# Stage changes with two chunks side by side, and three transposes on VectorE and a bounce through DRAM in place of TensorE

## The chip, the cores and the metric

One core of a Trainium2 chip runs the whole program. The metric is the device time of one execution in microseconds (us), smaller is better. It is the median of three executions; one more execution was recorded by the profiler, and all rows below are of that one.

## The reference

One layer of a streaming-encoder block on a sequence of 256 frames of 2048 float32 values. Everything is computed once, batch 1:

```python
h = rms_norm(x); p = h @ W_in                       # 2048 x 6656: [x_m | out gate | u | branch gates]
xc = silu(causal_conv(x_m)); q, k = xc @ Wq, xc @ Wk;  v = x_m @ Wv      # 4 heads of 256
hcell = mlstm(q, k, v, gates(q, k, v))              # matrix memory, max stabiliser
out  = sigmoid(out_gate) * (per_head_rms(hcell) * g + skip * xc)
y_m  = out @ W_up_m                                 # 1024 -> 2048
y    = s5(u); y = gelu(y); y = y * sigmoid(y @ W_glu + b)                # complex diagonal scan, 512 wide
y_s  = y @ W_up_s                                   # 512 -> 2048
x = x + (sigmoid(g_m) * y_m + sigmoid(g_s) * y_s) @ W_out
x = x + (silu(rms(x) @ W_gate) * (rms(x) @ W_up)) @ W_down               # 2048 -> 5632 -> 2048
out = rms_norm(x)
```

## The kernel before

Every large matrix is cut into blocks of 128 rows x 1024 columns (512 KB; two 128-row pieces of a 512-column chunk side by side). `emit_dma` loads a block by the SP queue into `raw` (3 buffers), `emit_split` makes `hi` (ScalarE, the cast of L156) and `lo = raw - hi` (VectorE, L94) of it (3 buffers each), and `o2_block` multiplies: 12 matmuls of 128x512 a block, hi by hi, lo by hi and hi by lo, for both halves (`tt`) of the sequence. The blocks run in one list: w_in in chunks of 8 blocks (`kp` 0 to 7) with the heads' v, q and k between them, the 2 blocks of w_glu inserted three blocks before the end of w_in, then w_up_s (8), w_up_m (16), w_out (32, four chunks), the FFN's gate and up chunks in turn (11 x (8 + 8), from block FFN0 = 168 on), and w_ffn_down (88). From block FFN0+4 on, every fourth block goes to a buffer of another pool, so that its load may be issued well ahead of its turn.

Two generators hold the work beside the blocks. `s5_gen` computes the S5 branch (the scan's products `bu` and `stm`, then `y_mm`, `gelu`, and `ghl`, the hi/lo halves of y). `ml_gen` computes the mLSTM branch (conv, gates, v, the heads, and at its end the output stage that makes `oh`/`ol`, the hi/lo pair that w_up_m multiplies). `pump` steps them between blocks; a yield gives the price by which it paces them. Whoever needs a result calls `until`: `glu_mm` for S5's y before w_glu, `ups_mm` for the GLU's result before w_up_s, `upm_mm` for `out` before w_up_m. After that a scheduler fixes the order of instructions on each engine. An engine takes its instructions strictly in that order.

A change of layout from frames on partitions to channels on partitions is done in two ways. v, the heads' output `hc` and the output gate `so` are transposed by TensorE with an identity (128x128 pieces, into PSUM `aux`). The gate products (`turn`) and the residual (`x1_T`) go by `blocks_T`, a VectorE transpose of 32x32 blocks (L274), and `groups_dma`, which stores the result to a DRAM tile `bounce` (one DMA) and loads it back in another order (four DMAs), all issued by GpSimd (POOL). After each w_out chunk, `x1_T(n)` also prepares `h2h`/`h2l`, that chunk's share of the FFN's left operand; the FFN's `kp` 6 and 7 read the share of chunk 3. In the same way w_out's `kp` 6 and 7 read the share of w_up_m's last chunk.

Of the kernel before, what the change touches and what calls it, by code (L numbers as in the profile page):

```python
# [17 lines left out]
P = 128  # L18
# [29 lines left out]
def block_kernel(ctx: ExitStack, tc: tile.TileContext, d, out):  # L48
# [18 lines left out]
    def u8(shape, dt=F32, name="u"):  # L67
        return up.tile(shape, dt, tag="u8", name=nm(name), bufs=NU8)
# [16 lines left out]
    def aux():  # L85
        return pp.tile([P, 512], F32, tag="aux", name=nm("aux"), bufs=4)
# [6 lines left out]
    def TT(o, a, b, op):  # L93
        return V.tensor_tensor(o, a, b, op=op)  # L94

    def STT(o, a, s, b, op0, op1, **kw):
        return V.scalar_tensor_tensor(out=o, in0=a, scalar=s, in1=b, op0=op0, op1=op1, **kw)  # L97

    def mm(o, l, r, start, stop):
        return PE.matmul(o, l, r, start=start, stop=stop, skip_group_check=True)  # L100
# [8 lines left out]
    def pvs(n, i=None, w=1):  # L109
        a, b = PV[n]  # L110
        if i is None:
            return pv[:, a:b]
        return pv[:, a + i : a + i + w]
# [164 lines left out]
    def groups_dma(dt_, st_):  # L278
# [3 lines left out]
        for j in range(4):  # L282
            nc.gpsimd.dma_start(  # L283
                dt_[32 * j : 32 * j + 32], bounce.rearrange("(i r) j x -> r i j x", i=4)[:, :, j]
            )


    s5 = {}

# [239 lines left out]
    def ml_gen():  # L529
# [38 lines left out]
        vk = u16([P, 2, 2048], name="vk")  # L568
        ml["vk"] = vk
        vtok = vk[:, 0].rearrange("p (a b) -> p a b", a=2)  # L570
        for st in range(2):
            for e4 in range(2):
                ps_ = aux()
                for e in range(4):
                    PE.transpose(ps_[:, e * 128 : e * 128 + 128], vT[:, e4 * 4 + e, st * 128 : st * 128 + 128], ident)
                A.copy(vtok[:, st, e4 * 512 : e4 * 512 + 512], ps_)
                yield 0.05, 0.45, e4
        gt = cp.tile([P, 2, 8], F32, name="gt")


# [5 lines left out]

        def gate_part(i, src, base):
            gs = m2([P, 256])
            nc.gpsimd.memset(gs, 0.0)
            ps_ = aux()  # L590
            for c in range(8):
                r = 32 * (c % 4)
                mm(ps_[r : r + 8, 0:256], wif[:, i * 8 + c, :], src[:, c, :], c < 4, c >= 4)
            for r in range(0, 128, 32):
                A.copy(gs[r : r + 8, :], ps_[r : r + 8, 0:256])
            yield 0.05, 1.2, 1
            pg = aux()
            for tt in range(2):
                mm(pg[:, tt * 8 : tt * 8 + 8], gs[:, tt * 128 : tt * 128 + 128], sel, True, True)
            TT(gt, pg[:, 0:16].rearrange("p (a b) -> p a b", a=2), base, ADD)  # L600
            yield 0.2, 0.4

        yield from gate_part(2, vT, pvs("bif").unsqueeze(1).broadcast_to([P, 2, 8]))
        del vT
        yield 0.2
        xch = u8([P, 8, 256], F32R, name="xch")
        xcl = u8([P, 8, 256], F32R, name="xcl")
# [14 lines left out]
        qT = ml["q"]  # L622
        yield from gate_part(0, qT, gt)
        yield 0.2
        while "k" not in state:
            yield 0
        yield 0.01, 0, 1
# [30 lines left out]
        for hp in range(2):  # L658
# [79 lines left out]
            yield 0.01, 0.65, 1  # L738
            for pT, h in zip(pTs, hh2):
                nps = aux()  # L740
                vs = lambda st: vtok[:, st, h * 256 : h * 256 + 256]
                mm(nps[:, 0:256], pT[:, 0], vs(0), True, True)
                mm(nps[:, 256:512], pT[:, 1], vs(0), True, False)
                mm(nps[:, 256:512], pT[:, 2], vs(1), False, True)
                for tt in range(2):
                    o = hc[:, 2 * h : 2 * h + 2, tt, :]
                    nv = nps[:, tt * 256 : tt * 256 + 256].rearrange("p (a b) -> p a b", a=2)
                    A.activation(o, nv, AF.Copy, scale=dinv[:, h, tt : tt + 1])
                    jk = m2([P, 2, 128])
                    A.activation(jk, o, AF.Square, accum_out=ssh[:, h, tt : tt + 1])  # L750
                yield 0.01, 1.3, 0
# [5 lines left out]
        for h in range(4):  # L757
            for tt in range(2):
                o = hc[:, 2 * h : 2 * h + 2, tt, :]
                A.activation(o, o, AF.Copy, scale=rsh[:, h, tt : tt + 1])  # L760
        yield 0.6, 0, 3
        while "win" not in state:
            yield 0
        so = ml["so"]
        oh = u8([P, 8, 256], F32R, name="oh")
        ol = u8([P, 8, 256], F32R, name="ol")
        for c2 in range(4):
            hps, sps = aux(), aux()
            for src, ps_ in ((hc, hps), (so, sps)):
                for cc in range(2):  # L770
                    for tt in range(2):
                        ct = 2 * c2 + cc
                        c = (cc * 2 + tt) * 128
                        PE.transpose(ps_[:, c : c + 128], src[:, ct, tt, :], ident)  # L774
            t = m2()
            for cc in range(2):
                ct = 2 * c2 + cc
                ts_ = t[:, cc * 256 : cc * 256 + 256]
                A.activation(ts_, xcT[:, ct, :], AF.Copy, scale=pvs("skip", ct))
                STT(ts_, hps[:, cc * 256 : cc * 256 + 256], pvs("mh", ct), ts_, MUL, ADD)  # L780
            TT(t, t, sps, MUL)
            v2 = lambda a: a[:, 2 * c2 : 2 * c2 + 2, :].rearrange("p a b -> p (a b)")
            A.copy(v2(oh), t)
            TT(v2(ol), t, f(v2(oh)), SUB)
            yield 2.1, 0.9, 1
        ml["out"] = (oh, ol)
        state["out"] = 1
        yield 0.1
# [11 lines left out]
    def win_evac(n, acc):  # L800
        if n == 4:
            ud = cp.tile([P, 4, 256], F32, name="s5ud")
            s5["ud"] = ud

            rb = s5["r1b"].rearrange("p (q c) -> p q c", c=16).unsqueeze(1).broadcast_to([P, 2, 16, 16])
            for h in range(2):
                o = ud[:, 2 * h : 2 * h + 2, :].rearrange("p a (q c) -> p a q c", c=16)
                TT(o, acc[h].rearrange("p (a c q) -> p a q c", a=2, q=16), rb, MUL)
            state["u"] = 1
        elif n < 2:  # L810
            if n == 0:
                ml["xm"] = u8([P, 2, 1024], name="xm")
            for tt in range(2):
                A.activation(
                    ml["xm"][:, tt, n * 512 : n * 512 + 512], acc[tt], AF.Copy, scale=r1[:, tt : tt + 1]
                )
            if n == 1:
                state["xm"] = 1
        elif n < 4:
            if n == 2:  # L820
                ml["so"] = u8([P, 8, 2, 128], name="so")
            for tt in range(2):
                A.activation(
                    ml["so"][:, 4 * (n - 2) : 4 * (n - 2) + 4, tt, :],
                    acc[tt].rearrange("p (a b) -> p a b", a=4),
                    AF.Sigmoid,
                    scale=r1[:, tt : tt + 1],
                )
            if n == 3:
                state["so"] = 1  # L830
        else:
            c = n - 5
            key, cc = ("gm", c) if c < 4 else ("gs", c - 4)
            if c == 0:
                mlg.until("heads")
            if cc == 0:
                cur[key] = u16([P, 2, 2048], name=key)
            bg = cur["bg"]
            for tt in range(2):
                o = gate_ap(key, tt, cc)  # L840
                STT(o, acc[tt], r1[:, tt : tt + 1], bg, MUL, ADD)
                A.activation(o, o, AF.Sigmoid)
# [145 lines left out]
    def out_mm(i, nk, hi, lo):  # L988
        n, kp = nk
        if n == 0 and kp == 0:  # L990
            cur["x1"] = u16([P, 2, 2048], name="x1")
            cur["h2h"] = [u8([P, 8, 256], F32R, name="h2h") for _ in range(2)]
            cur["h2l"] = [u8([P, 8, 256], F32R, name="h2l") for _ in range(2)]
        if kp == 0:
            cur["acc"] = [acc_tile(), acc_tile()]
            cs = slice(n * 512, n * 512 + 512)
            with tc.issue_after(wdma[0]):
                nc.sync.dma_start(cur["x1"][:, :, cs], d["x"].rearrange("(a p) c -> p a c", p=P)[:, :, cs])
        o2_block(cur["acc"], lhs_of(cur["mTh"], cur["mTl"], 8), (2 * kp, 2 * kp + 1), hi, lo, kp == 0, kp == 7)
        if kp == 7:  # L1000
            for tt in range(2):
                o = cur["x1"][:, tt, n * 512 : n * 512 + 512]
                TT(o, cur["acc"][tt], o, ADD)
                jk = t2()
                A.activation(jk, o, AF.Square, accum_out=ss2[:, tt, n : n + 1])
            later(lambda: x1_T(n))
# [147 lines left out]
        blocks.insert(len(blocks) - GLU, (d["w_glu"][0, b], glu_mm, (0, b)))  # L1154
    add_mat("w_up_s", 4, 2, ups_mm)
    add_mat("w_up_m", 4, 4, upm_mm)
    add_mat("w_out", 4, 8, out_mm)
    fg, fu = ffn_mm("fg"), ffn_mm("fu")
    FFN0 = len(blocks)
    for n in range(11):  # L1160
        for kp in range(8):
            blocks.append((d["w_ffn_gate"][n, kp], fg, (n, kp)))
        for kp in range(8):
            blocks.append((d["w_ffn_up"][n, kp], fu, (n, kp)))
    add_mat("w_ffn_down", 4, 22, down_mm)

    laters = []
# [187 lines left out]
```

## Time and profile before

| | us |
|---|---|
| median of 3 runs (1258.69 to 1264.71) | 1260.47 |
| profiled execution, its own time | 1258.85 |
| its span, first to last instruction | 1257.1 |
| TensorE (PE) busy | 1233.7 |
| VectorE (DVE) busy | 803.8 |
| ScalarE (ACT) busy | 604.0 |
| GpSimd (POOL) busy | 106.6 |

The span and the execution's own time differ by 1.75 us that lie outside the first and the last instruction. Busy shares are averages over stages; which engine is last in a stage is read from that stage. The mean granted clock of TensorE is 0.995 of full speed.

### The profile page before, as it was taken

To read this page: it belongs to the slowest core of one execution; us is meant where nothing else is said; L and a number is where in the kernel's file an instruction comes from. 1 tells how busy PE (TensorE), PEld (TensorE's weight loads), DVE (VectorE), ACT (ScalarE), POOL (GpSimd) and SP (SyncE) were. 2 spreads that over 40 slices of the span, in tenths; PEclk is the share of its full clock that TensorE was granted. 3 is DMA by queue.
4 is the path that set the end of the run, shared out by engine and by line. 5 is a ranking of instruction groups with operands and counts; after the bars stand their busy time and mean duration, and the time that the engine had idled before them with its cause. 6 is when DMAs were issued, how large, how long until landed. Compare 5 with 4: busy or idle time off the path is not lost.

```text
span 1257.1 us, 15683 instructions
## 1 busy us (share of the span) xinstructions
PE 1233.7 (98%) x5738; PEld 1015.3 (81%) x5738; DVE 803.8 (64%) x1162; ACT 604.0 (48%) x752; POOL 106.6 (8%) x199
## 2 busy tenths in 40 slices
PE   7999999999999999989999999999999999999997
PEld 7777888887788878868888888888888888888885
DVE  8779945999877856645556555555555554554544
ACT  7574554446654445444344444434444443444433
POOL 0000000000000522211101100110111010000000
PEclk9999999999999999989999999999999999999999
DMA  7645655554555977877667766555765686666443
GB/s 265 208 137 178 194 184 182 167 160 143 190 182 193 280 265 256 286 239 224 217 203 228 222 212 217 187 184 204 245 228 183 225 279 198 196 198 199 152 161 141
DMA packets 75597, 258.19 MB, mean 205 GB/s; under 512 B 10496, under 2 KB 11264, under 8 KB 75520
## 3 DMA queue, kind: packets, MB, share of 16 engines
q1 hardware_dynamic: 67616, 237.25, 58.1%
q0 software_dynamic: 7904, 19.94, 4.8%
q8 instruction: 45, 0.74, 0.2%
q14 instruction: 32, 0.26, 0.1%
HBM read 245.09 MB, written 12.06 MB: 205 GB/s over the span
## 4 chain that ended last, share of the span: by engine, by line
PE 85%; DVE 6%; DMA 5%; issue 2%; ACT 1%; ACTq 0%; SPq 0%; DVEq 0%
PE acc L100 80%; PE aux L100 4%; DMA raw<-in_w_out_dram 4%; DVE lo L94 3%; ACT hi L156 1%; DMA raw<-in_w_ffn_gate_dram 1%; DVE xcT L97 1%; DVE stm L94 0%; DVE bu L94 0%; DMA raw<-in_w_up_m_dram 0%; DVE x L94 0%; DVE gm L94 0%; DMA raw<-in_w_in_dram 0%; PE aux L774 0%; DVE h2l L97 0%
## 5 line engine op out<-in xcount | busy, mean ns | idle before, releaser
L94 DVE TENSOR_TENSOR lo<-raw,hi 128x1024 fp32r<-128x1024 f32 x427 | 521.0, 1221 | 403.6 <-ACT hi L156 403.0
L156 ACT CAST hi<-raw 128x1024 fp32r<-128x1024 f32 x427 | 449.1, 1053 | 577.5 <-PE acc L100 488.9
L100 PE MATMUL acc<-lo,h2h 128*128 128x512 f32 x704 | 275.2, 391 | 0.6 <-DVE lo L94 0.5
L100 PE MATMUL acc<-hi,h2l 128*128 128x512 f32 x704 | 274.2, 390 | 0.0
L100 PE MATMUL acc<-hi,h2h 128*128 128x512 f32 x704 | 246.8, 391 | 4.2 <-ACT hi L156 4.2
L100 PE MATMUL acc<-hi,aT 128*128 128x512 f32 x664 | 204.6, 389 | 0.0
L100 PEld LDWEIGHTS acc<-hi,h2h 128*128 128x128 f32 x704 | 132.5, 189 | 32.7 <-ACT hi L156 5.3
L100 PEld LDWEIGHTS acc<-lo,h2h 128*128 128x128 f32 x704 | 132.7, 189 | 29.6 <-DVE lo L94 2.1
L100 PE MATMUL acc<-lo,hTh 128*128 128x512 f32 x384 | 153.6, 400 | 1.3 <-DVE lo L94 1.2
L100 PEld LDWEIGHTS acc<-hi,h2l 128*128 128x128 f32 x704 | 132.8, 189 | 27.4
L100 PE MATMUL acc<-hi,hTl 128*128 128x512 f32 x384 | 150.4, 392 | 0.0
L100 PEld LDWEIGHTS acc<-hi,aT 128*128 128x128 f32 x664 | 124.7, 188 | 25.9
L100 PE MATMUL acc<-hi,hTh 128*128 128x512 f32 x384 | 139.4, 393 | 0.0
L100 PE MATMUL acc<-lo,aT 128*128 128x512 f32 x332 | 129.1, 389 | 0.0
L100 PEld LDWEIGHTS acc<-lo,hTh 128*128 128x128 f32 x384 | 72.1, 188 | 22.1 <-DVE lo L94 4.0
L100 PEld LDWEIGHTS acc<-hi,hTh 128*128 128x128 f32 x384 | 71.7, 188 | 16.7 <-issue 2.0
L100 PEld LDWEIGHTS acc<-hi,hTl 128*128 128x128 f32 x384 | 72.2, 188 | 14.6 <-issue 0.7
L281 POOL DMA_DIRECT2D bounce<-m x30 | 16.9, 565 | 690.5 <-DVE m L274 690.2
L100 PEld LDWEIGHTS acc<-lo,aT 128*128 128x128 f32 x332 | 62.3, 188 | 12.9
L283 POOL DMA_DIRECT2D m<-bounce x120 | 65.6, 554 | 43.1 <-DMA bounce<-m 28.2
L100 PE MATMUL acc<-lo,mTh 128*128 128x512 f32 x128 | 50.0, 392 | 0.0
L100 PE MATMUL acc<-hi,mTl 128*128 128x512 f32 x128 | 49.5, 389 | 0.0
(246 smaller groups left out, 1077.7 us busy)
## 6 DMA issues: line engine op xcount, KB each, us to landing
raw<-in_w_in_dram SPq DMA_DIRECT2D x104, 512.0 KB, 3.5
raw<-in_w_ffn_gate_dram SPq DMA_DIRECT2D x88, 512.0 KB, 3.7
raw<-in_w_ffn_up_dram SPq DMA_DIRECT2D x88, 512.0 KB, 4.2
raw<-in_w_ffn_down_dram SPq DMA_DIRECT2D x88, 512.0 KB, 3.5
raw<-in_w_out_dram SPq DMA_DIRECT2D x32, 512.0 KB, 5.0
raw<-in_w_up_m_dram SPq DMA_DIRECT2D x16, 512.0 KB, 3.6
bounce<-m POOLq DMA_DIRECT2D x30, 256.0 KB, 4.1
m<-bounce POOLq DMA_DIRECT2D x120, 64.0 KB, 4.2
```

What stands on the lines that cost most here:

```text
L94: return V.tensor_tensor(o, a, b, op=op)
L97: return V.scalar_tensor_tensor(out=o, in0=a, scalar=s, in1=b, op0=op0, op1=op1, **kw)
L100: return PE.matmul(o, l, r, start=start, stop=stop, skip_group_check=True)
L156: A.copy(hi, raw)
L281: nc.gpsimd.dma_start(bounce, st_)
L283: nc.gpsimd.dma_start(dt_[32 * j : 32 * j + 32], bounce.rearrange("(i r) j x -> r i j x", i=4)[:, :, j])
```

## The change

1. A new helper `bounce_T` does a VectorE transpose into a small tile and then `groups_dma` on it. v (4 calls, now after the first gate part), the heads' output (`hcd`, 4 calls) and the output gate (4 calls, in the evacuation of w_in's chunks 2 and 3) go through it. The 48 TensorE transposes and the 4 ScalarE copies of v go. The heads' matmul and the output stage read the new layout by strides; the output stage's 4 multiplications of 512 columns become 8 of 256. Three small memsets move from GpSimd to VectorE.
2. The prices in the yields of the output stage and around it change.
3. w_out's chunks 0 and 1 run side by side (kp 0 to 5 of both, then kp 6 and 7 of both), each with its own pair of accumulators; the FFN's first gate and up chunks do the same.

```diff
+    def bounce_T(o, i):
+        st_ = m2([P, 4, 4, 32])
+        V.transpose(st_.rearrange("p j a c -> p a j c"), i.rearrange("p a (j c) -> p a j c", j=4))
+        groups_dma(o.rearrange("p (i x) -> p i x", i=4), st_.rearrange("p j a c -> p j (a c)"))
...
-        for st in range(2):
-            for e4 in range(2):
-                ps_ = aux()
-                for e in range(4):
-                    PE.transpose(ps_[:, e * 128 : e * 128 + 128], vT[:, e4 * 4 + e, st * 128 : st * 128 + 128], ident)
-                A.copy(vtok[:, st, e4 * 512 : e4 * 512 + 512], ps_)
-                yield 0.05, 0.45, e4
...
-            nc.gpsimd.memset(gs, 0.0)
+            V.memset(gs, 0.0)
...
+        for st in range(2):
+            for e4 in range(2):
+                bounce_T(vtok[:, st, e4 * 512 : e4 * 512 + 512], vT[:, 4 * e4 : 4 * e4 + 4, st * 128 : st * 128 + 128])
+                yield 0.75
...
-        yield 0.6, 0, 3
+        yield 0.6, 0, 1
+        hcd = u8([P, 2, 2, 512], name="hcd")
+        for hh in range(2):
+            for tt in range(2):
+                bounce_T(hcd[:, hh, tt], hc[:, 4 * hh : 4 * hh + 4, tt, :])
+                yield 0.75
+        yield 0.01, 0, 3
...
-            hps, sps = aux(), aux()
-            for src, ps_ in ((hc, hps), (so, sps)):
-                for cc in range(2):
-                    for tt in range(2):
-                        ct = 2 * c2 + cc
-                        c = (cc * 2 + tt) * 128
-                        PE.transpose(ps_[:, c : c + 128], src[:, ct, tt, :], ident)
...
-                STT(ts_, hps[:, cc * 256 : cc * 256 + 256], pvs("mh", ct), ts_, MUL, ADD)
-            TT(t, t, sps, MUL)
+                tv = ts_.rearrange("p (i c) -> p i c", c=32)
+                STT(tv, dv_(hcd, ct), pvs("mh", ct), tv, MUL, ADD)
+                TT(tv, tv, dv_(so, ct), MUL)
...
-            yield 2.1, 0.9, 1
+            yield 2.4, 0, 0
...
+                sg = t2()
+                A.activation(sg, acc[tt], AF.Sigmoid, scale=r1[:, tt : tt + 1])
+                bounce_T(ml["so"][:, n - 2, tt], sg.rearrange("p (a c) -> p a c", a=4))
...
-    add_mat("w_out", 4, 8, out_mm)
+    SPLIT = 6
+    for ms, a, b in (((0, 1), 0, SPLIT), ((0, 1), SPLIT, 8), ((2, 3), 0, 8)):
+        for m in ms:
+            for kp in range(a, b):
+                blocks.append((d["w_out"][m, kp], out_mm, (m, kp)))
...
+        for a, b in ((0, SPLIT), (SPLIT, 8)) if n == 0 else ((0, 8),):
+            for kp in range(a, b):
+                blocks.append((d["w_ffn_gate"][n, kp], fg, (n, kp)))
+            for kp in range(a, b):
+                blocks.append((d["w_ffn_up"][n, kp], fu, (n, kp)))
```

How the instructions move, in three places. First VectorE, around the second half of S5's y (`ghl`, row with `s5ud,ghl`), on which the second block of w_glu waits. Before, it comes behind the lo of w_glu's second block (`lo_3207`); the two lo behind it belong to w_in's chunk 8, kp 5 and 6:

```order
L94 TENSOR_TENSOR lo_3167<-raw_3094,hi_3166 128x1024
L94 TENSOR_TENSOR t_3263<-t_3263,s5ud 128x512
L94 TENSOR_TENSOR ghl_3271<-s5ud,ghl_3271 128x512
L94 TENSOR_TENSOR lo_3189<-raw_3116,hi_3188 128x1024
L97 SCALAR_TENSOR_TENSOR t_3263<-t_3263,s5ud 128x512
L94 TENSOR_TENSOR lo_3207<-raw_3136,hi_3206 128x1024
L94 TENSOR_TENSOR ghl_3271<-s5ud,ghl_3271 128x512
L94 TENSOR_TENSOR lo_3232<-raw_3164,hi_3231 128x1024
L94 TENSOR_TENSOR lo_3305<-raw_3186,hi_3304 128x1024
L94 TENSOR_TENSOR s5ud<-s5ud,sgt_3270 128x512
```

In the change (`lo_3284`, `lo_3382` and `lo_3416` are of w_in's chunk 8, kp 5 to 7, `lo_3436` and `lo_3460` of w_up_s, `m` is the output stage, `bu` the S5 scan's last product):

```order
L94 TENSOR_TENSOR lo_3284<-raw_3213,hi_3283 128x1024
L94 TENSOR_TENSOR m_3674<-m_3674,so_2184 128x256 x2
L94 TENSOR_TENSOR bu_668<-bu_668,stm_930 128x64x15
L94 TENSOR_TENSOR lo_3382<-raw_3231,hi_3381 128x1024
L94 TENSOR_TENSOR lo_3416<-raw_3259,hi_3415 128x1024
L97 SCALAR_TENSOR_TENSOR s5ud<-s5ud,pv,aux_3330 128x256
L91 TENSOR_SCALAR t_3340<-t_3340 128x512
L94 TENSOR_TENSOR t_3340<-t_3340,s5ud 128x512
L94 TENSOR_TENSOR lo_3436<-raw_3281,hi_3435 128x1024
L97 SCALAR_TENSOR_TENSOR t_3340<-t_3340,s5ud 128x512
L94 TENSOR_TENSOR lo_3460<-raw_3379,hi_3459 128x1024
L94 TENSOR_TENSOR ghl_3348<-s5ud,ghl_3348 128x512
```

The second half of y now stands behind five more lo, the whole of the output stage's multiplications and the last scan product. Then TensorE at the start of w_up_s. Before, the last matmuls of w_in stand between w_glu and w_up_s, and the transposes of `hc` stand in w_up_s's first block:

```order
L100 MATMUL acc_3123<-hi_3338,hTh_79 128x512
L100 MATMUL acc_3123<-lo_3339,hTh_79 128x512
L100 MATMUL acc_3123<-hi_3338,hTl_81 128x512
L100 MATMUL acc_3408<-hi_3358,ghl_3271 128x512
L100 MATMUL acc_3409<-hi_3358,ghl_3271 128x512
L774 MATMUL aux_3482<-cst,hc_2214 128x128 x4
L100 MATMUL acc_3408<-lo_3359,ghl_3271 128x512
L100 MATMUL acc_3408<-hi_3358,ghl_3271 128x512
```

In the change the rows ahead of w_up_s (`acc_3485`) are the last ones of w_glu's second block (`aux_3354`):

```order
L100 MATMUL aux_3354<-ghl_3348,hi_3261 128x256 x2
L100 MATMUL aux_3354<-ghl_3348,lo_3262 128x256
L100 MATMUL aux_3354<-ghl_3348,hi_3261 128x256 x2
L100 MATMUL aux_3354<-ghl_3348,lo_3262 128x256
L100 MATMUL acc_3485<-hi_3435,ghl_3348 128x512
L100 MATMUL acc_3485<-lo_3436,ghl_3348 128x512
L100 MATMUL acc_3486<-hi_3435,ghl_3348 128x512
L100 MATMUL acc_3486<-lo_3436,ghl_3348 128x512
```

All of w_in is done ahead of w_glu's second block, the transposes are gone, and w_up_s has only that block in front of it. Last the SP queue at the FFN's start, before (the first row is gate, kp 4; the five behind it are loads for later blocks; then gate kp 5 and 6 and the up chunk):

```order
L144 DMA raw_4702<-in_w_ffn_gate_dram 128x1024
L144 DMA raw_4788<-in_w_ffn_gate_dram 128x1024
L144 DMA raw_4868<-in_w_ffn_up_dram 128x1024
L144 DMA raw_4950<-in_w_ffn_up_dram 128x1024
L144 DMA raw_5022<-in_w_ffn_gate_dram 128x1024
L144 DMA raw_5117<-in_w_ffn_gate_dram 128x1024
L144 DMA raw_4726<-in_w_ffn_gate_dram 128x1024
L144 DMA raw_4758<-in_w_ffn_gate_dram 128x1024
L144 DMA raw_4806<-in_w_ffn_up_dram 128x1024
```

and in the change:

```order
L144 DMA raw_4743<-in_w_ffn_gate_dram 128x1024
L144 DMA raw_4829<-in_w_ffn_up_dram 128x1024
L144 DMA raw_4909<-in_w_ffn_up_dram 128x1024
L144 DMA raw_4983<-in_w_ffn_up_dram 128x1024
L144 DMA raw_5063<-in_w_ffn_gate_dram 128x1024
L144 DMA raw_5158<-in_w_ffn_gate_dram 128x1024
L144 DMA raw_4767<-in_w_ffn_gate_dram 128x1024
L144 DMA raw_4799<-in_w_ffn_up_dram 128x1024
L144 DMA raw_4847<-in_w_ffn_up_dram 128x1024
```

The load of gate kp 5 keeps its place behind five loads for later blocks; behind it now come blocks of the up chunk, and gate kp 6 and 7 later.

## Rows read from the trace of the kernel before

**Rows 1.** The page, parts 1 and 4: busy time of the engines, and the chain's shares.
```profile
PE 1233.7 (98%) x5738; PEld 1015.3 (81%) x5738; DVE 803.8 (64%) x1162; ACT 604.0 (48%) x752; POOL 106.6 (8%) x199
PE 85%; DVE 6%; DMA 5%; issue 2%; ACT 1%; ACTq 0%; SPq 0%; DVEq 0%
```

**Rows 2.** Waits of TensorE: waiter, releaser, total us, times, longest.
```profile
PE acc L100 <- ACT hi L156: 12.6, 4, 6.8
PE acc L100 <- DVE lo L94: 1.7, 2, 1.2
```

**Rows 3.** The chain that ended last: start us, us, what.
```profile
142.56 0.87 PE aux L575 x8
...
349.60 5.27 PE aux L100 x44
354.87 3.20 PE acc L100 x14
...
442.75 5.64 DMA raw<-in_w_out_dram
...
527.15 9.94 DMA raw<-in_w_ffn_gate_dram
...
546.57 701.64 PE acc L100 x3094
```

**Rows 4.** Groups by line: the transposes on TensorE.
```profile
L774 PE MATMUL aux<-cst,so 128*128 128x128 f32 x16 | 2.6, 272 | 0.0
L575 PE MATMUL aux<-cst,vT 128*128 128x128 f32 x16 | 2.4, 272 | 0.0
```

**Rows 5.** Windows: us; busy us and count of PE, PEld, DVE, ACT, POOL; clock, DMA share, GB/s.
```profile
447.00:450.00 3.00, 1.48 (x7) 0.86 (x5) 1.66 (x2) 2.31 (x3) 0.47 (x1) 1.00 0.85 264
535.00:549.00 14.00, 9.24 (x26) 5.97 (x26) 6.39 (x8) 5.69 (x8) 4.36 (x8) 0.76 0.80 278
322.00:371.00 49.00, 49.00 (x263) 39.91 (x262) 39.57 (x50) 32.76 (x45) 0.00 (x0) 1.00 0.56 184
```

**Rows 6.** The chain within 520 to 560 us: the start of the FFN.
```profile
537.19 1.05 ACT hi L156
...
539.54 4.65 PE acc L100 x10
```

**Rows 7.** Groups by line: VectorE's operations of this case.
```profile
L94 DVE TENSOR_TENSOR lo<-raw,hi 128x1024 fp32r<-128x1024 f32 x17 | 20.8, 1221 | 5.3 <-ACT hi L156 5.3
L94 DVE TENSOR_TENSOR bu<-bu,stm 128x960 f32<-128x960 f32 x3 | 3.4, 1149 | 0.0
L97 DVE SCALAR_TENSOR_TENSOR m<-aux,pv,m 128x256 f32<-128x256 f32 x8 | 3.5, 478 | 0.5 <-PE aux L774 0.5
L94 DVE TENSOR_TENSOR m<-s5c,s5sm 128x256 f32<-128x256 f32 x4 | 1.6, 419 | 0.0
L94 DVE TENSOR_TENSOR ol<-m,oh 128x512 fp32r<-128x512 f32 x4 | 2.7, 683 | 0.0
L274 DVE STREAM_TRANSPOSE x1sd<-x 128x512 f32<-128x512 f32 x8 | 5.3, 692 | 0.0
```

**Rows 8.** VectorE's timeline: start us, us, instruction, idle before it.
```profile
321.00 1.22 DVE L94 TENSOR_TENSOR lo<-raw,hi 128x1024 fp32r<-128x1024 f32 x1
...
348.87 0.69 DVE L94 TENSOR_TENSOR ghl<-s5ud,ghl 128x512 fp32r<-128x512 f32 x1 [0.45 <-ACT ghl L508]
...
360.26 0.69 DVE L94 TENSOR_TENSOR ghl<-s5ud,ghl 128x512 fp32r<-128x512 f32 x1
...
368.05 1.23 DVE L94 TENSOR_TENSOR lo<-raw,hi 128x1024 fp32r<-128x1024 f32 x1 [0.98 <-ACT hi L156]
```

**Rows 9.** Matmuls that read ghl: durations ns, first and last start us.
```profile
L100 PE MATMUL acc<-hi,ghl x64: 387/389/477, 363.5 to 387.8; 128*128 128x512 f32 x64
```

**Rows 10.** DMA issues of the bounce: KB each, median us to landing.
```profile
bounce<-m POOLq DMA_DIRECT2D x30, 256.0 KB, 4.1
m<-bounce POOLq DMA_DIRECT2D x120, 64.0 KB, 4.2
```

More of the change, by code (lines that the diff above doesn't have):

```diff
@@ L603, in ml_gen @@
         yield from gate_part(2, vT, pvs("bif").unsqueeze(1).broadcast_to([P, 2, 8]))
-        del vT
         yield 0.2
@@ L624, in ml_gen @@
         yield 0.2
+        for st in range(2):
+            for e4 in range(2):
+                bounce_T(vtok[:, st, e4 * 512 : e4 * 512 + 512], vT[:, 4 * e4 : 4 * e4 + 4, st * 128 : st * 128 + 128])
+                yield 0.75
+        del vT
         while "k" not in state:
@@ L740, in ml_gen @@
                 nps = aux()
[L741 to L744, printed above, removed]
+                vs = lambda st: vtok[:, st, (h // 2) * 512 : (h // 2) * 512 + 512].rearrange(
+                    "p (i a c) -> p a i c", i=4, a=4
+                )[:, 2 * (h % 2) : 2 * (h % 2) + 2]
+                no = lambda t: nps[:, t * 256 : t * 256 + 256].rearrange("p (a i c) -> p a i c", a=2, i=4)
+                mm(no(0), pT[:, 0], vs(0), True, True)
+                mm(no(1), pT[:, 1], vs(0), True, False)
+                mm(no(1), pT[:, 2], vs(1), False, True)
                 for tt in range(2):
@@ L766, in ml_gen @@
         ol = u8([P, 8, 256], F32R, name="ol")
+        dv_ = lambda d_, ct: d_[:, ct // 4].rearrange("p t (i a c) -> p a (t i) c", i=4, a=4)[:, ct % 4]
         for c2 in range(4):
-            hps, sps = aux(), aux()
-            for src, ps_ in ((hc, hps), (so, sps)):
-                for cc in range(2):
-                    for tt in range(2):
-                        ct = 2 * c2 + cc
-                        c = (cc * 2 + tt) * 128
-                        PE.transpose(ps_[:, c : c + 128], src[:, ct, tt, :], ident)
             t = m2()
@@ L820, in win_evac @@
             if n == 2:
-                ml["so"] = u8([P, 8, 2, 128], name="so")
+                ml["so"] = u8([P, 2, 2, 512], name="so")
             for tt in range(2):
[L823 to L828, printed above, removed]
+                sg = t2()
+                A.activation(sg, acc[tt], AF.Sigmoid, scale=r1[:, tt : tt + 1])
+                bounce_T(ml["so"][:, n - 2, tt], sg.rearrange("p (a c) -> p a c", a=4))
             if n == 3:
@@ L994, in out_mm @@
         if kp == 0:
-            cur["acc"] = [acc_tile(), acc_tile()]
+            cur["out", n] = [acc_tile(), acc_tile()]
             cs = slice(n * 512, n * 512 + 512)
@@ L998, in out_mm @@
                 nc.sync.dma_start(cur["x1"][:, :, cs], d["x"].rearrange("(a p) c -> p a c", p=P)[:, :, cs])
-        o2_block(cur["acc"], lhs_of(cur["mTh"], cur["mTl"], 8), (2 * kp, 2 * kp + 1), hi, lo, kp == 0, kp == 7)
+        o2_block(cur["out", n], lhs_of(cur["mTh"], cur["mTl"], 8), (2 * kp, 2 * kp + 1), hi, lo, kp == 0, kp == 7)
         if kp == 7:
@@ L1002, in out_mm @@
                 o = cur["x1"][:, tt, n * 512 : n * 512 + 512]
-                TT(o, cur["acc"][tt], o, ADD)
+                TT(o, cur["out", n][tt], o, ADD)
                 jk = t2()
@@ L1160, in block_kernel @@
     for n in range(11):
[L1161 to L1164, printed above, removed]
+        for a, b in ((0, SPLIT), (SPLIT, 8)) if n == 0 else ((0, 8),):
[3 more added lines that the diff above has]
+                blocks.append((d["w_ffn_up"][n, kp], fu, (n, kp)))
     add_mat("w_ffn_down", 4, 22, down_mm)
```

## The prediction

> **What bounds the kernel now.** I read the page first. TensorE is busy for 1233.7 of 1257.1 us and the chain that ended last runs through it for 85% [rows 1]; behind 546.57 us that chain is one piece of 3094 matmuls, 0.2268 us each [rows 3]. So time can be won in three ways only: less work on TensorE, shorter waits of TensorE, and a higher clock while it works. The waits of its matmuls add up to 14.3 us, of which the longest, 6.8 us, is the start of the kernel [rows 2]; the change doesn't touch that one. The windows tell where the others lie: at 447 to 450 us, where w_out begins, and at 535 to 549 us, where the FFN begins [rows 5]. The third window of that group is the reader's warning: from 322 to 371 us TensorE never idles, but VectorE is busy for 39.57 of the 49 us [rows 5]. There is little room for more work on VectorE in that stretch, and the change puts more there.
>
> **The transposes.** Eight of v's took 0.87 us of TensorE, 0.109 us each [rows 3]; the record of one is longer, 272 ns, because they overlap [rows 4]. 48 of them are 5.2 us. With what TensorE loses in turning to them and back it may be a little more; I take 5.2. In their place VectorE gets 12 transposes of 128x512, 0.692 us each in the nearest row [rows 7], 8.3 us, and the POOL queue 12 bounces. A bounce lands about 4.1 + 4.2 = 8.3 us after its issue, plus the issues [rows 10]; POOL is busy for 106.6 us in all [rows 1], and each of the three results is wanted later than that by the order of instructions, so I take 0. If a bounce came late, its 8.3 us would be the bound. Four copies less on ScalarE, three memsets on VectorE (nothing to under 0.7 us each, the price of a whole 512-column operation [rows 7]) and the strided operands of the heads' matmuls and the output stage I take at 0, since the nearest rows are the same operations; if the output stage's 16 strided operations ran at half speed, they would add some 7 us to VectorE (8 x 0.478 + 8 x 0.419 [rows 7]), which I keep for the upper end.
>
> Here a rule speaks against the change. By the row, a transpose costs TensorE 0.109 us [rows 3], and the same columns on VectorE cost 0.692 / 4 = 0.173 us [rows 7]. The Trainium skill (VectorE: DVE Perf Modes, Rules for kernel authors) says to use TensorE for a 128x128 transpose where a result in PSUM will do, and that VectorE transposes only blocks of 32x32. The row's prices rank the two engines' work as that rule does; by TensorE's share alone the exchange would give 5.2 us back, by the rule it would be a loss of up to 8.3 us wherever VectorE is last. Which of the two holds is a question of place, and the next step answers it.
>
> **VectorE before w_up_s.** The order of instructions shows what the new yields do: S5's remainder falls behind the mLSTM's output stage. I count VectorE's instructions from the lo that starts at 321.00 us before (w_in chunk 7, kp 5) to the lo of the fourth w_up_s block (368.05 before) [rows 8]. Up to the first of them the two kernels have about the same work: up to twelve transposes more (0.69 us each), eight steps of the S5 scan less (1.15 us each [rows 7]). Between the two, both have 16 lo. The change has 4 `bu` and 4 `stm` more (8 x 1.149 = 9.2 us), 4 scalar products of the output stage more (4 x 0.478 = 1.9), 8 products of 256 columns in place of one of 512 (8 x 0.419 - 0.68 = 2.7), and 3 `ol` more (3 x 0.683 = 2.0): 15.8 us by records [rows 7]. Records overlap a little; the 0.08 us or so by which one instruction starts before the last one's record ends leave about 14. Added to 39.57 us of 49 that is about 54: five us too many even if VectorE never waited [rows 5]. If its waits of today (9.4 us) all stayed, it would be 14 to 16 us too many. So the lateness lies between 5 and 16 us.
>
> To choose I walk along the second half of `ghl`, for which w_glu's second block waits. It starts at 348.87 us before [rows 8]. In the change, 14 lo stand between the anchor and it instead of 9, and with the products above 48 us of records, 45 us of work, instead of 24: from 322 us on it ends at 367 at the earliest. Then follow w_glu's 24 matmuls, 5.27 / 44 x 24 = 2.9 us [rows 3], and what comes between the last of w_glu's matmuls and the second half of the next `ghl`: 354.87 to 360.95 before, 6.1 us [rows 3, 8]. Before, three blocks of w_in covered that (they begin at 354.87 [rows 3]); now they run ahead of w_glu's second block. So w_up_s is in full work at about 376 us where it began at 363.5 [rows 9]: 12 us late. TensorE waits for these us in several pieces, at the lo of w_in's last chunk and at w_glu. I take 12. The 24 transposes that stood behind the start of w_up_s still save 2.6 us then; the other 24 are swallowed, since in this stretch VectorE sets the pace and not TensorE.
>
> **The two stage changes.** At w_out's start TensorE stands still for 1.5 of 3 us [rows 5], for a cast whose block was loaded late (issued at 442.75, 5.64 us [rows 3]); with the waits for lo beside it the loss is 1.9 us. It is chunk 1's first block, which TensorE takes ahead of chunk 0's kp 6 and 7, whose operand from w_up_m's last chunk comes late. In the new list chunk 1's blocks are loaded two places earlier, and kp 6 and 7 have 12 blocks in front of them; I take the whole 1.9.
>
> At the FFN's start 14 us hold 26 matmuls [rows 5]; at 0.2268 us they take 5.9 us, so 8.1 us are lost. In parts: gate kp 5 is loaded in 9.94 us [rows 3], behind five loads for later blocks, and its cast comes at 537.19 [rows 6]. Then the next ten matmuls take 4.65 us, 0.465 each, about twice the usual [rows 6]; the clock of the window is 0.76 of full speed [rows 5], the lower of two levels, 1.2 instead of 2.4 GHz, in half of it. Then a third wait, for kp 6, because chunk 3's share is not ready. The side-by-side order puts six blocks of 2.7 us in front of kp 6, so the last wait goes. The first is uncertain: five loads still stand ahead of gate kp 5 on the queue. But the lo that lets it issue no longer stands behind the residual's work, which was about 2 us. I take 7 of the 8.1, with 5 as the lower bound.
>
> **The sum.** 1258.85 + 12.0 (w_up_s late) - 2.6 (transposes behind it) - 1.9 (w_out) - 7.0 (FFN) = 1259.4. To this I add one stretch at the lower clock behind a wait of about 3 us, priced by the one stretch that is shown: ten matmuls in 4.65 instead of 2.27 us [rows 6], 2.4 us. That gives 1261.8, or **1262 us**, 1.5 above the median of the runs shown, whose profiled execution stands 1.6 below it.
>
> **Rivals.** *VectorE keeps up (faster).* If VectorE's waits vanish wholly, the lateness is 5 us: 1258.85 + 5 - 2.6 - 1.9 - 7 = 1252. If the S5 remainder were hidden altogether, all 48 transposes count: 1258.85 - 5.2 - 1.9 - 8.1 = 1244. For it: TensorE never waited in this stretch before although VectorE had 39.57 of 49 us [rows 5]. Against it: 14 more us don't fit into 9.4.
>
> *The lower clock (slower).* The new waits of TensorE come one behind another between 335 and 376 us, each of 1 to 5 us. The one wait of some 3 us in the middle of the kernel was followed by ten matmuls at half pace [rows 6]. If four new waits do the same, 4 x 2.4 = 9.6 us are added in place of 2.4: 1269; with the lateness at 16 us 1273. This decides as soon as more than three such stretches appear. The Trainium skill (TensorE: Matmul & The Clock Gate, HAM oscillation) describes just this: waits between bursts of matmuls send the engine back to its lower clock, and the price is paid anew each time. The window at the FFN's start agrees with it once, at 0.76 [rows 5].
>
> *The stage change does not do its work.* If gate kp 5 waits as before behind the five loads, and the clock falls there as before, only 1 to 2 of the 8.1 us come back: 1258.85 + 12 - 2.6 - 1.9 - 1.5 + 2.4 = 1267. For it: the queue's order at that place is unchanged.
>
> **How the numbers follow.** About 0.5%, 6.3 us, is what a measurement of this kernel can tell from no change. My forecast, gains and lateness near balance (1254 to 1267), has 0.40. VectorE keeping up, 1244 to 1254, has 0.33. The lower clock has 0.16 and the stage change that does nothing 0.11, together 1266 to 1276. From these: faster 0.34, same 0.39, slower 0.27. The range 1246 to 1272 leaves out the lowest part of the second case and the highest of the third, about 0.2; the forecast's own range is 1256 to 1267.
>
> **What would show it.** Right: in the profile after, waits of TensorE for VectorE (`lo`, `ghl`) between 335 and 380 us of some 12 us, w_up_s beginning at about 373 to 376, no wait at w_out's start, at most 2 us at the FFN's, no rows of L575 and L774. Wrong, if VectorE idles before w_glu, if w_up_s begins before 368, or if the window at the FFN's start still shows a clock near 0.76.

## The result, and the profile after

The changed kernel takes 1270.22 us (1269.42 to 1271.01) where the kernel before takes 1260.46: ratio 1.0072, 95% interval 1.0055 to 1.0089. It is slower by 9.8 us, inside the range that was given and 8 us above the predicted time. It lies outside the forecast's own range (1256 to 1267), in the band that the two slower rivals shared (1266 to 1276), and 0.7% is past the 0.5% that the prediction called no change: of its three outcomes "slower" had the lowest chance, 0.27. The profiled execution took 1269.42 us, its span is 1267.6 us.

The page's first part, engines' busy time, stands against [rows 1]; the rows under it are the waits of TensorE, against [rows 2].

```profile
PE 1235.4 (97%) x5690; PEld 1014.6 (80%) x5690; DVE 812.1 (64%) x1181; ACT 601.6 (47%) x748; POOL 138.8 (11%) x256
```
```profile
PE acc L100 <- ACT hi L156: 12.0, 3, 7.0
PE acc L100 <- ACT ghl L526: 4.5, 1, 4.5
PE acc L100 <- DVE lo L94: 3.3, 5, 1.2
PE aux L100 <- ACT ghl L514: 3.2, 1, 3.2
PE aux L100 <- DVE ghl L94: 0.5, 1, 0.5
```

TensorE has 48 instructions fewer, yet its busy time has grown: a matmul at the lower clock is busy for longer (records of 0.63 us behind 379.2 us, 0.39 at full clock). Three of these rows are new: the waits for `ghl`, which holds the hi and lo of S5's y (L514 and L94) and then of the GLU's result (L526). The waits for lo have grown from 1.7 to 3.3 us, and the cast wait of 3.9 us at the FFN's start is among the first row's. The windows (columns as in [rows 5]) show where the time goes.

```profile
322.00:371.00 49.00, 43.19 (x207) 32.87 (x206) 45.86 (x60) 25.45 (x34) 10.38 (x19) 0.95 0.67 206
366.00:379.00 13.00, 5.33 (x26) 4.75 (x26) 8.28 (x12) 8.68 (x15) 0.00 (x0) 0.76 0.26 82
378.60:402.60 24.00, 24.00 (x97) 19.64 (x98) 14.25 (x17) 7.90 (x8) 0.00 (x0) 0.91 0.47 152
460.00:470.00 10.00, 10.00 (x46) 8.29 (x45) 6.00 (x6) 5.26 (x6) 1.58 (x3) 1.00 0.82 263
546.00:560.00 14.00, 10.07 (x30) 7.25 (x30) 5.79 (x7) 5.94 (x9) 2.91 (x6) 0.76 0.86 273
```

Between 322 and 371 us VectorE is now busy for 45.86 of 49 us (39.57 before) and TensorE does 207 matmuls instead of 263. Where w_out's chunk 1 begins, 18 us behind w_out's first matmul in both kernels (449.6 before, about 464 now), there is no wait left. At the FFN's start 14 us hold 30 matmuls at a clock of 0.76; before it was 26 at the same 0.76.

VectorE's timeline around the second half of `ghl` answers to [rows 8]. Each row: start, us, instruction, and the idle time before it.

```profile
360.95 1.23 DVE L94 TENSOR_TENSOR lo<-raw,hi 128x1024 fp32r<-128x1024 f32 x1 [0.90 <-ACT hi L156]
362.09 0.48 DVE L97 SCALAR_TENSOR_TENSOR s5ud<-s5ud,pv,aux 128x256 f32<-128x256 f32 x1
363.27 0.43 DVE L91 TENSOR_SCALAR t<-t 128x512 f32<-128x512 f32 x1 [0.70 <-ACT t L469]
...
369.24 0.69 DVE L94 TENSOR_TENSOR ghl<-s5ud,ghl 128x512 fp32r<-128x512 f32 x1
374.31 0.69 DVE L94 TENSOR_TENSOR s5ud<-s5ud,sgt 128x512 f32<-128x512 f32 x1 [4.38 <-ACT sgt L933]
```

The second half of y comes at 369.24 us; it was 348.87 [rows 8]. TensorE's timeline shows what stands still for it: w_glu's second block waits 3.19 us, its matmuls then run at half pace at first (clock 0.65 from 369.26 to 374.12), and w_up_s waits 4.47 us for the product of w_glu, with nothing in between to fill the time.

```profile
369.26 1.31 PE L100 MATMUL aux<-ghl,hi 128*128 128x256 f32 x3 [3.19 <-ACT ghl L514]
...
373.84 0.28 PE L100 MATMUL aux<-ghl,lo 128*128 128x256 f32 x1
378.59 0.80 PE L100 MATMUL acc<-hi,ghl 128*128 128x512 f32 x1 [4.47 <-ACT ghl L526]
```

The chain (start, us, what) leaves VectorE at 352.1, where TensorE begins most of w_glu's first block. From there it runs through TensorE (but for one lo at 356.04, 1.15 us), up to w_in's last blocks, and then through ScalarE to the second half of y. From w_glu's end to w_up_s ScalarE carries it: its four casts of `oh`, the output stage's, stand ahead of the cast of `ghl`.

```profile
351.50 0.61 DVE ghl L94
...
352.15 3.89 PE aux L100 x18
...
360.86 5.23 PE acc L100 x22
366.16 1.04 ACT hi L156
...
368.70 0.52 ACT ghl L514
...
373.81 0.47 ACT sgt L933
374.28 2.06 ACT oh L790 x4
376.34 0.94 ACT hi L156
377.28 0.74 ACT sgt L933 x2
378.03 0.52 ACT ghl L526
```

So w_up_s begins at 378.59 instead of 363.53 us [rows 9], 15.1 us late. w_up_m begins 14.5 us late (402.57 against 388.07), w_out's first matmul the same, the FFN's first 11.9 us late (533.13 against 521.19) and the last matmul ends 10.6 us late (1258.75 against 1248.19). From one of these places to the next the lateness changes by +15.1, -0.6, -2.6 and -1.4 us: 10.5 in all.

### The profile page after: what moved, and what is told of

Its sections match the earlier page's. It is cut to its first block, busy times and chain, and to the rows that moved or that the text cites. A ratio compares the mean times of both kernels' runs of the same rounds, so it can differ in the third digit from the quotient of the medians.

```text
span 1267.6 us, 15719 instructions
## 1 busy us (share of the span) xinstructions
PE 1235.4 (97%) x5690; PEld 1014.6 (80%) x5690; DVE 812.1 (64%) x1181; ACT 601.6 (47%) x748; POOL 138.8 (11%) x256
## 4 chain that ended last, share of the span: by engine, by line
PE 88%; DVE 6%; DMA 2%; issue 1%; ACT 1%; SPq 0%; ACTq 0%; DVEq 0%
PE acc L100 83%; PE aux L100 4%; DVE lo L94 2%; DMA raw<-in_w_ffn_gate_dram 1%; DVE bu L94 1%; DVE stm L94 1%; DVE xcT L97 1%; ACT hi L156 1%; DMA raw<-in_w_in_dram 0%; DMA raw<-in_w_out_dram 0%; DVE m L97 0%; DVE hTl L97 0%; DVE xcT L94 0%; ACT oh L790 0%; DVE x L94 0%
## 5 line engine op out<-in xcount | busy, mean ns | idle before, releaser
L94 DVE TENSOR_TENSOR lo<-raw,hi 128x1024 fp32r<-128x1024 f32 x427 | 521.3, 1222 | 396.8 <-ACT hi L156 395.9
L281 POOL DMA_DIRECT2D bounce<-m x42 | 23.6, 563 | 762.3 <-DVE m L274 479.8
```

The source lines that it names most:

```text
L281: nc.gpsimd.dma_start(bounce, st_)
```

## The experiments

Each run is compared with executions of the kernel before that were taken with it on the same chip; differences from the kernel before are medians against those. Their medians lie between 1258.92 and 1260.13 us. The changed kernel was not measured again beside the runs: where one is set against it, its 1270.22 us stands, and such a difference is uncertain by about 1 us.

**The stage part alone**, on the kernel before:

```diff
-    add_mat("w_out", 4, 8, out_mm)
+    SPLIT = 6
+    for ms, a, b in (((0, 1), 0, SPLIT), ((0, 1), SPLIT, 8), ((2, 3), 0, 8)):
+        ...
```

> The kernel before with the side-by-side order of w_out and the FFN's first chunks alone; all transposes stay on TensorE. Theory (the loss of the change lies ahead of w_up_s, and the stage part gains what it gained in the changed kernel, 2.6 us at w_out and 1.4 us at the FFN): about 1256.5 us, 4 us under before, with the wait for the load of gate kp 5 still there (3 to 4 us). Rival (the FFN part gains 7 us once the bounces are gone): about 1251 us, and no wait over 2 us at the FFN's start.

1254.03 against 1260.13 us, ratio 0.9948 (0.9931 to 0.9965): 6 us faster, halfway between the two expectations. In its trace the FFN's first matmul comes 2.6 us earlier than in the kernel before and the last matmul another 2.7 us earlier. The wait for gate kp 5 is still 3.07 us long, as the theory had it; the third wait, 1.13 us before, is gone. The first row holds the kernel's start (6.9 us) and the wait for gate kp 5:

```profile
PE acc L100 <- ACT hi L156: 10.0, 2, 6.9
PE acc L100 <- DVE lo L94: 1.7, 2, 1.2
```

**The bounces with the new prices**, w_out and the FFN in the old order:

```diff
-    SPLIT = 6
-    for ms, a, b in (((0, 1), 0, SPLIT), ((0, 1), SPLIT, 8), ((2, 3), 0, 8)):
...
+    add_mat("w_out", 4, 8, out_mm)
```

> The change without its stage part: v, the heads' output and the output gate by VectorE and the bounce, w_out and FFN in the old order. Theory: w_up_s begins some 15 us late as in the changed kernel, so about 1274 to 1275 us, 14 us over before. Rival (the loss comes from both parts together, for instance from their DMA traffic): 1264 to 1268 us.

1280.21 against 1260.13 us, ratio 1.0159 (1.0134 to 1.0184): 20 us slower, more than either expectation. w_up_s and w_up_m begin 16.9 and 16.6 us late, as the theory had it. But then another 4.7 us are lost behind w_up_m, 2.8 in w_out and 1.9 in the FFN, in more waits than before, most of them under 1.2 us, as its waits of TensorE show against [rows 2]:

```profile
PE acc L100 <- ACT hi L156: 14.6, 6, 6.9
PE acc L100 <- DVE lo L94: 8.5, 12, 2.2
```

So the bounces and their prices lose, and the stage part takes back more beside them (20 - 10 = 10 us) than alone (6). Why w_out in the old order meets more waits here than in the kernel before was not tested, and no run changes the prices without the bounces.

**The FFN's early loads in the order of the blocks**, in the changed kernel:

```diff
+            if FFN0 + 4 <= i < FFN0 + 24 and i % 4 == 3:
+                with tc.issue_after(wdma[0]):
+                    wdma[0] = nc.sync.dma_start(raw, blocks[i][0]).ins
```

> The changed kernel, but the early loads of the FFN's first 24 blocks are issued in the order of the blocks, so that the load of gate kp 5 stands directly behind that of kp 4. Theory (those five loads make gate kp 5 late): the wait of 3.9 us and the stretch at the lower clock behind it go, 6 us less than the changed kernel, about 1264 us. Rival (the DMA engines are full there whatever the order): the wait moves to a neighbouring block, 1269 to 1271 us.

1263.95 against 1260.13 us, ratio 1.0031 (1.0019 to 1.0044): 6 us less than the changed kernel (5 by the two ratios), as the theory had it. The chain runs through the FFN's start in one piece; in the changed kernel it went through the load (second fence, the changed kernel's).

```profile
523.10 37.06 PE acc L100 x162
```
```profile
538.27 11.32 DMA raw<-in_w_ffn_gate_dram
...
549.69 1.05 ACT hi L156
...
550.78 1.22 PE acc L100 x2
```

From the FFN's first matmul to the end of the last one that reads `h2h` it takes 479.1 us, 486.0 in the changed kernel and 487.4 in the kernel before.

**The same edit on the kernel before**, nothing else changed:

> The kernel before with the FFN's early loads in the order of the blocks and nothing else; the stage order is the old one. Theory (the wait for gate kp 5 and the slow matmuls behind it come from the five loads ahead of it, the later wait for kp 6 from chunk 3's share): the wait of 3.1 us goes, the one for kp 6 stays or grows by about 1 us, 1255 to 1257 us. Rival (the waits have one cause, chunk 3's share, and a block loaded earlier only waits longer for it): 1259 to 1261 us.

1255.78 against 1258.92 us, ratio 0.9971 (0.9957 to 0.9985). The wait for gate kp 5 is gone, the later one is left at 1.13 us: two waits with two causes, the loads' order for the first and the order of the blocks for the other, which the run with the stage part alone took away. That chunk 3's share lies behind the second is an argument from the order of instructions (below).

**S5's remainder earlier**, in the changed kernel, by the pacing alone:

```diff
-SLACK = 0.3
+SLACK = 0.0
```

> The changed kernel with the constant SLACK of the pacing at 0 instead of 0.3, so that the side work, S5's remainder with it, is issued earlier: the second half of y stands behind nine lo fewer on VectorE than in the changed kernel; no work is added or removed. Theory (the order is what makes w_up_s late, not the amount of work): w_up_s begins 2 us before the time of the kernel before or thereabouts, and the whole comes to 1254 to 1257 us. Rival (VectorE has too much work in any order): the waits move ahead of w_in's last chunks and the time stays within 3 us of the changed kernel, 1267 to 1273 us.

1251.31 against 1260.13 us, ratio 0.992 (0.9895 to 0.9946): some 19 us less than the changed kernel. The operations are the same; only their order on the engines is another. By the order of instructions, 12 of the output stage's 16 products stand behind the second half of y here, too. The window of 322 to 371 us and the matmuls that read `ghl`:

```profile
322.00:371.00 49.00, 48.81 (x238) 41.10 (x237) 41.04 (x58) 35.04 (x52) 10.90 (x20) 1.00 0.75 238
```
```profile
L100 PE MATMUL acc<-hi,ghl x64: 389/389/389, 363.8 to 385.3; 128*128 128x512 f32 x64
```

TensorE waits for 0.2 us there, w_up_s begins at 363.8 and ends 2.5 us earlier than before: the 24 transposes behind its start, 2.6 us. The amount of work was not what made the change slow.

**The output stage behind S5's remainder**, S5 as late as in the changed kernel:

```diff
-PACE = [(0,24,1.0),(24,80,0.1),(80,140,0.5)]
+PACE = [(0,24,1.0),(24,80,0.1),(80,140,1.0)]
```

> The changed kernel with the pacing's share at 1.0 for S5 from block 80 on: the 16 products of the output stage move behind S5's remainder, but the second half of y still stands behind as many lo. Theory (everything ahead of the second half of y on VectorE counts by its time): the products' 6 to 7 us come back, w_up_s begins about 9 us late instead of 15, 1263 to 1265 us. Rival (what is late is only the scan, and the products lay in VectorE's waits): 1269 to 1271 us.

1261.41 against 1259.93 us, ratio 1.0001 (0.9983 to 1.0018). w_up_s begins at 373.0 us, 9.5 late instead of 15.1, as the theory had it. The time fell by some 2 us more than expected: the wait ahead of w_up_s became shorter (2.2 instead of 4.5 us; the casts of `oh` no longer stand ahead of the cast of `ghl`), and the one at the FFN's start too (2.6 instead of 3.9).

```profile
L100 PE MATMUL acc<-hi,ghl x64: 389/389/628, 373.0 to 396.3; 128*128 128x512 f32 x64
```

**v on TensorE again**, the other two transposes by the bounce:

```diff
-                bounce_T(vtok[:, st, e4 * 512 : e4 * 512 + 512], vT[:, 4 * e4 : 4 * e4 + 4, st * 128 : st * 128 + 128])
-                yield 0.75
...
+                    PE.transpose(ps_[:, e * 128 : e * 128 + 128], vT[:, e4 * 4 + e, st * 128 : st * 128 + 128], ident)
+                A.copy(vtok[:, st, e4 * 512 : e4 * 512 + 512], ps_)
+                yield 0.05, 0.45, e4
```

> The changed kernel with v transposed by TensorE again, at its old place and price in the pacing; the heads' output and the output gate keep the bounce. The second half of y then stands behind 3 lo fewer and 4 transposes fewer. Theory: w_up_s begins 5 to 7 us earlier than in the changed kernel, less 1.7 us for 16 transposes on TensorE where it doesn't wait: 1264 to 1267 us. Rival (the output stage's own products alone make the lateness): 1269 to 1272 us.

1257.91 against 1259.93 us, ratio 0.9983 (0.9968 to 0.9999): lower than both expectations. w_up_s begins at 369.1, 9.5 us earlier than in the changed kernel where 5 to 7 were expected. By the order of instructions the last scan product stands behind 5 lo fewer on VectorE, too, and 4 of the output stage's 16 products behind the second half of y, which the estimate did not count: without v's price the pacing issues S5 earlier. The FFN's wait is 1.2 us here.

```profile
L100 PE MATMUL acc<-hi,ghl x64: 389/389/796, 369.1 to 392.4; 128*128 128x512 f32 x64
```

**Both repairs together**, and then the same two with all transposes, and with v's alone, on TensorE (the edit of v as above, or the stage part on the kernel before):

```diff
-SLACK = 0.3
+SLACK = 0.0
...
+            if FFN0 + 4 <= i < FFN0 + 24 and i % 4 == 3:
+                with tc.issue_after(wdma[0]):
```

> The changed kernel with both repairs, the earlier S5 remainder (SLACK 0) and the FFN's early loads in the order of the blocks. Theory (two separate places): the gains add, 1251.3 less the 3.2 us of the remaining wait and the slow matmuls behind it, about 1246 us, and no wait of TensorE over 1.5 us from the start of w_out on. Rival (the load order is hidden anyway once S5 is early): 1250 to 1252 us.

> The same two repairs and the stage part, but all 48 transposes stay on TensorE. It gives the worth of the exchange where VectorE is not late. Theory (5.2 us less on TensorE count in full there): 5 us over the run with both repairs and the bounces, about 1251 us. Rival (the bounces' gain is eaten by waits for VectorE elsewhere): within 2 us of that run.

> Both repairs, the stage part and the bounces of the heads' output and the output gate, but v transposed by TensorE. v's 16 transposes lie where VectorE sets the pace, so that their 1.7 us on TensorE don't show and VectorE is relieved of 4 transposes. Theory: 1246 to 1248 us, the run with both repairs or up to 1.5 us less. Rival (v's 1.7 us on TensorE count in full): 1249 to 1250 us.

1247.80 against 1259.93 us with all bounces, ratio 0.9904 (0.9879 to 0.9929); 1249.84, ratio 0.9919 (0.9895 to 0.9944), with all transposes on TensorE; 1246.89 against 1258.92, ratio 0.9896 (0.9869 to 0.9922), with v's there. The two repairs add nearly in full: 1251.3 less 3.5 us, and no wait over 1.5 us is left behind the kernel's start. The waits of TensorE in that run, with all bounces (the cast is at L160 there):

```profile
PE acc L100 <- ACT hi L160: 8.0, 2, 7.7
PE acc L100 <- DVE lo L94: 3.9, 6, 1.2
```

The exchange of transposes is worth 2 us there, as the rival had it, not 5.2, and the intervals overlap: w_up_s begins at the same time with the bounces (365.0) as without (365.2), so the 24 transposes ahead of it give nothing, and the 24 behind give 2.9 us, of which 1.4 are lost again by the time the FFN begins. The fastest version, with v on TensorE, is within the intervals of the one with all bounces.

## Why the prediction was right or wrong

**VectorE before w_up_s: right in kind, 3 us short.** The forecast lateness was 12 us, 15.1 were measured, between the bounds of 5 and 16. The prices held. Groups by line, of after, against [rows 7]:

```profile
L97 DVE SCALAR_TENSOR_TENSOR m<-hcd,pv,m 128x256 f32<-128x256 f32 x8 | 3.3, 480 | 0.0
L94 DVE TENSOR_TENSOR m<-m,so 128x256 f32<-128x256 f32 x8 | 2.9, 421 | 0.0
L290 DVE STREAM_TRANSPOSE m<-vT 128x512 f32<-128x512 f32 x4 | 2.8, 709 | 2.8 <-DMA bounce<-m 2.8
L290 DVE STREAM_TRANSPOSE m<-hc 128x512 f32<-128x512 f32 x4 | 2.6, 686 | 0.0
L100 PE MATMUL aux<-vk,m 128*128 128x256 f32 x24 | 5.8, 378 | 0.0
```

Strided operands cost nothing that shows against those rows: 480 and 421 ns against 478 and 419, and the matmuls group that holds the heads' product with v is at 378 ns, 379 before. (The row of 478 read its operand from PSUM, so that this pair is not alike in all but the strides.) The bounces, too, were taken at nothing, and TensorE waits for none of them; VectorE waits once, 2.8 us for a buffer, at 155 us and far ahead of this stretch. The walk's 45 us of work for VectorE held, too: from the lo at its start (322.70) to the end of the second half of y (369.93) it is busy for 45.15 us. But the walk let it work without a wait. That is so up to 352.1; behind it VectorE waits for 2.1 us, 0.90 of them for a cast that had waited for TensorE.

Against the walk, w_glu's second block begins 2.3 us late (369.26 instead of 367). It takes 4.86 us instead of 2.9, at a clock of 0.65 behind a wait of 3.19 us: another 2.0. From its end to w_up_s 4.47 us pass instead of 6.1, 1.6 less. With the 0.5 us by which 376 was rounded down to 12 us late, that is the 3 us. The casts of `oh` lie in the 4.47 us. That the order, not the amount, is the cause is shown by the run with S5 earlier. The run that moved the output stage brought back 5.6 us (15.1 to 9.5): w_glu's second block begins 4.4 us earlier there (364.90), takes 1.1 longer, and w_up_s follows it after 2.2 us instead of 4.5.

**The transposes behind w_up_s: 0.6 instead of 2.6 us.** The 24 transposes are gone, but 96 matmuls took 24.0 us (window of 378.60 to 402.60, clock 0.91) where 0.2268 us each make 21.8: the 2.2 us of slow matmuls behind the wait of 4.47 us ate most of them.

**w_out: 2.6 instead of 1.9 us.** The wait went, as forecast, and 0.7 us more.

**The FFN's start: the step that failed.** The prediction took 7 of the 8.1 us, and said that the first wait was uncertain; 1.4 us came. The wait for gate kp 5 did not shrink from 3.07 but grew to 3.89 us: its load took 11.32 us where it took 9.94 [rows 3], and the stretch at the lower clock behind it stayed (window clock 0.76 in both). What went is the third wait, of 1.13 us. TensorE's and ScalarE's timelines, before, and last the changed kernel's wait:

```profile
538.28 1.22 PE L100 MATMUL acc<-hi,h2h 128*128 128x512 f32 x2 [3.07 <-ACT hi L156]
544.22 1.04 ACT L156 CAST hi<-raw 128x1024 fp32r<-128x1024 f32 x1 [3.80 <-PE acc L100]
545.17 1.70 ACT L1027 ACTIVATE h2h<-x1sd,pv 128x256 fp32r<-128x256 f32 x4
545.31 0.74 PE L100 MATMUL acc<-hi,h2h 128*128 128x512 f32 x2 [1.13 <-ACT hi L156]
```
```profile
550.78 1.22 PE L100 MATMUL acc<-hi,h2h 128*128 128x512 f32 x2 [3.89 <-ACT hi L156]
```

The prediction called it the wait for kp 6. By the order of instructions it is the wait for the up chunk's first block, which TensorE takes behind gate kp 5, ahead of gate kp 6 and 7. The hi of kp 6 and 7 hold two of the three buffers until chunk 3's share comes (`h2h`, from 545.17 on), so the up block's cast has to wait for gate kp 5's last matmul. So the rival "the stage change does not do its work" came true at this place, with its price (1.5 us given there). Of the 2 us that were to come because the lo that lets the load issue stands earlier, 0.8 came: the load was issued 5.1 us behind the FFN's first matmul, 6.0 before, and landed later all the same. The run with the loads in order shows that the five loads were the cause.

**The clock.** One slow stretch was priced, 2.4 us. Three new ones came, behind waits of 1.06 and 0.46 us (w_glu's first block at 352), of 3.19 and of 4.47 us; they cost 1.8, 2.0 and 2.2 us. The fourth, behind the 3.89 us at the FFN's start, stood in the kernel before, too. A window in the first of them:

```profile
353.00:355.00 2.00, 2.00 (x12) 2.00 (x11) 2.00 (x3) 0.00 (x0) 0.00 (x0) 0.50 0.59 225
```

The rival of the lower clock was to decide with more than three such stretches. There are four, and the three new ones cost 6.0 us, where it had 9.6. That its 1269 us is so near to the measured time is luck: its sum still holds the 7 us at the FFN's start that did not come. The Trainium skill (TensorE: Matmul & The Clock Gate, HAM oscillation) describes matmul bursts parted by waits for loads, with the price paid anew at each; the three waits of over 3 us agree with it. The shorter ones go both ways: 1.06 and 0.46 us were followed by a clock of 0.50, while the kernel before kept 1.00 at w_out, where TensorE stood still for 1.5 us [rows 5].

**The sum.** 1258.85 + 15.1 - 0.6 - 2.6 - 1.4 = 1269.4, the profiled execution's own time. By the forecast's terms it was 12 + 2.4 - 2.6, 1.9 and 7: the FFN is 5.6 us of the 7.6 that it lay too low, the transposes are 2.0, the lateness with its slow stretch 0.7, and w_out gave 0.7 more than forecast.

**The signs.** Of the signs of being right, two came: no wait at w_out's start, and no rows of L575 and L774. Between 335 and 380 us TensorE waits for 10.3 us instead of some 12, but only 1.6 of them are put down to VectorE; the rest are put down to ScalarE's casts. w_up_s begins later than the 373 to 376 us given, and the FFN's wait is 3.9 us instead of at most 2. One sign of being wrong came as it was named: the window at the FFN's start still shows a clock of 0.76. So the time lies in the range and the loss lies ahead of w_up_s, as forecast, but the step at the FFN was wrong.

## What to carry to other kernels

Before work is moved from the engine that is busy for 98% to one that is busy for 64%, look at the one stretch where the second engine is nearly full, and walk along the chain that ends there: here the same instructions gave 1270 or 1251 us, by their order alone. A price in a planner's table does more than pace its own step; it can push back whatever shares the budget, as v's price did with the S5 scan. And a load that is issued early for later blocks can hold back the load that is wanted next, here at a price of 3 us in the kernel before and 6 in the changed kernel: read the queue's order at a stage change, not only the order of the matmuls.

## What the runs showed that was not expected

A wait of 2.2 us ahead of w_up_s was also followed by slow matmuls: with v on TensorE the window behind it has a clock of 0.84, and the one at the FFN's start, behind waits of 1.2 and 0.5 us, 0.79:

```profile
369.00:380.00 11.00, 10.89 (x41) 8.59 (x42) 7.06 (x9) 5.51 (x8) 0.00 (x0) 0.84 0.43 144
538.00:546.00 8.00, 7.25 (x24) 5.53 (x25) 4.84 (x5) 4.50 (x8) 2.32 (x5) 0.79 0.89 280
```

In the kernel before with the loads in order, waits of 1.1 and 0.5 us at the same place left the clock at full speed:

```profile
538.00:548.00 10.00, 8.34 (x36) 6.25 (x35) 5.14 (x8) 5.54 (x8) 0.00 (x0) 1.00 0.73 233
```

So the length of one wait alone does not tell whether the clock falls. What else decides was not tested.
